# A planner that counts TensorE's instructions as ready some time behind their operands, in a hybrid attention and gated-MLP layer

## The chip, the cores and the metric

One core of one Trainium2 chip runs the whole layer as one program. The metric is the device time in microseconds (us), from the first to the last instruction with what lies around it. The engines are named as the profile names them: PE is TensorE (PEld its weight loads), DVE is VectorE, ACT is ScalarE, POOL is GpSimd, and SP issues the transfers. Each engine runs its own list of instructions strictly in order and waits for the others by semaphores.

## What is computed

The reference is one decoder layer over 2048 positions of 1024 numbers, in float32:

```
h = rmsnorm(x); qkv = h @ w_qkv
group A (4 heads): softmax(q1 k1) - lam * softmax(q2 k2), times v, per-head norm
group B (8 heads of 64): z = q k / 8;  beta = sigmoid(z);  1 - beta = sigmoid(-z)
     weight of key j = beta_j * product over later keys of (1 - beta);  out = weights @ v
x = x + rmsnorm(concat(A, B) @ w_o)
u = causal_conv3(rmsnorm(x) @ w_up);  x = x + rmsnorm((gelu(gate) * val) @ w_down)
```

The kernel keeps float32 accuracy on PE by splitting each operand into a rounded part (hi) and its rest (lo), and by three matmuls for hi*hi, hi*lo and lo*hi; in the heads two matmuls do where the hi and lo of one operand lie side by side.

## The kernel before

**The order of the work is made by a planner.** The program first records every piece of work as an `Op`, with its engine, an estimated duration, the operations it depends on and the buffers it takes. `Plan.run` (line 180 on) then plays this list through: at each moment it gives every idle engine the ready operation of the best priority whose buffers are free, and it writes out the instruction right there. So the planner's clock has no effect on the chip except one: it fixes the order in which the instructions of each engine stand. An operation counts as ready 200 ns (`LAT`) after the end of an operation of another engine that it needs, or 60 ns (`SAME`) after one of its own engine.

**The stages.** Up to about 750 us the program computes norms, the q/k/v projection (lines 603 and 606, tile `g`, weights `big`, activations `hT`) and the differential heads of group A. Each step of the projection is a row of six matmuls of 256 columns. Then come the stick-breaking heads of group B (`sb_stream`, line 929 on), in units of 512 queries by up to 512 keys, together with the rest of the projection as filler. The output projection (`wo_block`, line 1126 on, tiles `mt` and `g`, matmuls in line 1141) takes over as filler where the heads run out, and the MLP (`up` line 1266, `dn` line 1351) ends the program.

**One unit of group B** has four rows of 128 queries. For each row PE makes the scores `z` (line 959, with the mask of line 962 on the diagonal), ACT makes two sigmoids (lines 965 and 967), DVE a running product (the scan of line 973) and POOL the product of both (line 977). Then `tstep` transposes the four rows for one block of 128 keys on PE (line 989, four transposes into tile `t`), ACT or DVE rounds them (`thi`, lines 467 and 468), DVE takes the rest (`tlo`, line 996), and PE multiplies both by v into tile `o` (line 1012, first the `thi`, then the `tlo`). There are two buffers each for `t`, `thi` and `tlo`, so the transposes after next can be placed only behind the matmul that reads the present `tlo`.

Of the kernel before, what the change touches and what calls it, by code (L numbers as in the profile page):

```python
# [70 lines left out]


class Op:
    __slots__ = ("ways", "eng", "bufs", "prio", "left", "ready", "succ", "start", "end", "nbytes", "what")

    def alt(self, eng, dur, fn):

# [75 lines left out]
class Plan:  # L153
# [6 lines left out]
    QUEUE = 3000.0  # L160

    def __init__(self):
        self.ops, self.now = [], 0.0

    def op(self, eng, dur, fn, deps=(), bufs=(), lead=0.0, nbytes=0, what=None):
        o = Op()
        o.ways, o.eng, o.nbytes, o.what = {eng: (dur, fn)}, None, nbytes, what
        o.bufs = list(dict.fromkeys(bufs))
        for b in o.bufs:
            b.left += 1  # L170
            b.tag.ops.append(o)
        o.prio = (self.now - lead, len(self.ops))
        o.left, o.ready, o.succ, o.start, o.end = 0, 0.0, [], None, None
        for d in dict.fromkeys(deps):
            d.succ.append(o)
            o.left += 1
        self.ops.append(o)
        return o

    def run(self):  # L180
# [15 lines left out]
        while events:  # L196
# [9 lines left out]
            while again:  # L206
                again = False
                for e in engines:
# [6 lines left out]
                    for i, o in enumerate(ready[e]):  # L215
                        if any(b.held > t and b.by != e for b in o.bufs):
                            continue
                        new = [b for b in o.bufs if b.mem is None]
                        got = []
                        for b in new:  # L220
                            if not b.tag.fits(b):
                                break
                            b.tag.take(b)
                            got.append(b)
                        if len(got) < len(new):
                            for b in got:
                                b.tag.undo(b)
                            continue
                        for a in o.ways:
                            ready[a].remove(o)  # L230
                        dur, fn = o.ways[e]
                        o.eng = e
                        again = True
                        left -= 1
                        fn()
                        o.start = t
                        if e == "SP":
                            dma = max(dma, t + 1600) + o.nbytes / 250.0
                            o.end = dma + 1300
                            busy[e] = t + 475  # L240
                        else:
                            o.end = t + dur
                            busy[e] = o.end if e is not None else t
                        if busy[e] > t:
                            at(busy[e], "n", None)
                        for s in o.succ:
                            s.left -= 1
                            s.ready = max(s.ready, o.end + (self.SAME if list(s.ways) == [e] else self.LAT))
                            if s.left == 0:
                                at(s.ready, "r", s)  # L250
                        for b in o.bufs:
                            b.left -= 1
                            b.done = max(b.done, o.end)
                            if b.tag.bank and b.left:
                                b.held, b.by = o.end + self.BANK, e
                                at(b.held, "n", None)
                            if b.left == 0:
                                at(b.done + 100, "f", b)
                        break
# [7 lines left out]
def layer_kernel(  # L267
# [412 lines left out]
    def load_kv(g, c):  # L680
        cs = slice(c * 512, (c + 1) * 512)
        kt, v = buf("k"), buf("v")
        tiles = (2 * c, 2 * c + 1)
        assert all(kstore[g, i] and vstore[g // 2, i] for i in tiles)
        ok = load(lambda: f32(kt.t), kd[g][:, :, cs], 1 << 19, (kt,), [o for i in tiles for o in kstore[g, i]],
                  what="kload")
        ov = load(lambda: f32(v.t), vd[g // 2][g % 2, c], 1 << 19, (v,),
                  [o for i in tiles for o in vstore[g // 2, i]], what="vload")
        kv[g, c] = (kt, v, ok, (ov,))
# [728 lines left out]
    run(with_setup(qkv_steps(0, 2, 4)))  # L1418
    load_q(0, 0)
    load_kv(0, 0)  # L1420
    for mark, p, i0, i1 in (((0, 2), 0, 4, 6), ((0, 4), 0, 6, 8),
# [4 lines left out]
        run(merge(until(heads, *mark), qkv_steps(p, i0, i1)))  # L1426
    wo_weights()
    run(merge(until(heads), chain.from_iterable(wo_block(b) for b in range(8))))
    for b in range(8, NB):
        run(wo_block(b))  # L1430
    ffn_all()
    plan.run()

# [35 lines left out]
```

## Time and profile before

| | |
|---|---|
| median of 3 runs | 3116.48 us (3113.1 to 3118.24) |
| the profiled execution | 3117.43 us, its span 3115.6 us |
| PE busy | 2999.2 us, 96% |
| DVE busy | 2231.4 us, 72% |
| ACT, POOL busy | 1437.6 us (46%), 932.5 us (30%) |

The shares are means over stages that differ: DVE is idle much of the MLP and nearly full in group B. The profile also names, for each idle stretch of an engine, the instruction that ended it. A matmul's record can be longer than the time that it costs, because matmuls overlap.

### The profile page before, as it was taken

How to read it: one execution, taken by the hardware profiler on the slowest of the kernel's cores; microseconds unless marked ns; L12 is line 12 of the kernel's file. 1: busy time of each engine (PE TensorE's matmuls, PEld its weight loads, DVE VectorE, ACT ScalarE, POOL GpSimd, SP SyncE). 2: the span in 40 equal slices, each digit the busy share in tenths (PEclk: the TensorE clock that was granted, in tenths of full speed). 3: DMA queues.
4: the chain of work that ended last, by engine and by line, in shares of the span. 5: the costliest groups of instructions: out<-in, count | busy, mean ns of one | idle time of the engine just before them, and what ended most of it. 6: DMA issues, size and time to landing. Idle time of an engine off the chain costs nothing. (4 is left out here: it accounts for less than half of the span.)

```text
span 3115.6 us, 46750 instructions
## 1 busy us (share of the span) xinstructions
PE 2999.2 (96%) x16840; PEld 2586.1 (83%) x16840; DVE 2231.4 (72%) x4230; ACT 1437.6 (46%) x2873; POOL 932.5 (30%) x1008
## 2 busy tenths in 40 slices
PE   7999999999989998989999999999999999999998
PEld 7898999999878887867777888888888888888887
DVE  4658878897999898999755764377734776267742
ACT  4434545555676676766653433233422433233321
POOL 1011002002686675755422111033301332023310
PEclk9999999999999999999999999999999999999999
DMA  7775657655634355532263333343344333343332
GB/s 245 263 216 163 189 157 200 179 142 169 188 112 146 116 162 177 159 107 94 92 220 130 100 101 116 117 134 95 95 128 142 96 101 105 115 140 101 95 122 81
DMA packets 383965, 437.01 MB, mean 140 GB/s; under 512 B 20112, under 2 KB 311796, under 8 KB 373492
## 3 DMA queue, kind: packets, MB, share of 16 engines
q1 hardware_dynamic: 383732, 434.02, 46.1%
q8 instruction: 132, 2.16, 0.3%
q14 instruction: 101, 0.83, 0.1%
HBM read 333.27 MB, written 100.67 MB: 139 GB/s over the span
## 5 line engine op out<-in xcount | busy, mean ns | idle before, releaser
L1266 PE MATMUL pu<-fh,fhi 128*128 128x512 f32 x2816 | 868.2, 389 | 0.0
L1266 PEld LDWEIGHTS pu<-fh,fhi 128*128 128x128 f32 x2816 | 528.9, 188 | 110.4
L462 DVE TENSOR_TENSOR flo<-fraw,fhi 128x1024 fp32r<-128x1024 f32 x190 | 237.5, 1250 | 504.3 <-ACT fhi L459 504.0
L1266 PE MATMUL pu<-fh,flo 128*128 128x512 f32 x1408 | 548.2, 389 | 0.0
L977 POOL TENSOR_TENSOR ring_w<-ring_w,ring_a 128x512 f32<-128x512 f32 (+2 forms) x320 | 411.6, 1297 | 238.1 <-DVE ring_a L973 127.6
L459 ACT CAST fhi<-fraw 128x1024 fp32r<-128x1024 f32 x254 | 267.3, 1053 | 419.2 <-PE py L1351 248.0
L606 PE MATMUL g<-hT,big 128*128 128x256 f32 x3072 | 448.7, 288 | 8.1 <-DVE st L625 4.2
L1351 PE MATMUL py<-fhi,gt 128*128 128x512 f32 x1408 | 440.8, 393 | 0.0
L606 PEld LDWEIGHTS g<-hT,big 128*128 128x128 f32 x3072 | 412.2, 192 | 22.7 <-DVE st L625 5.6
L973 DVE TENSOR_TENSOR_SCAN ring_a<-ring_a 128x513 f32<-128x513 f32 (+2 forms) x320 | 408.0, 1295 | 7.4 <-ACT ring_a L965 6.6
L467 ACT CAST thi<-t 128x512 fp32r<-128x512 f32 (+3 forms) x422 | 215.5, 518 | 255.3 <-PE t L989 127.1
L1351 PEld LDWEIGHTS py<-fhi,gt 128*128 128x128 f32 x1408 | 264.3, 188 | 66.0
L1266 PEld LDWEIGHTS pu<-fh,flo 128*128 128x128 f32 x1408 | 264.4, 188 | 55.4
L460 POOL TENSOR_TENSOR flo<-fraw,fhi 128x1024 fp32r<-128x1024 f32 x74 | 186.0, 2514 | 356.8 <-ACT fhi L459 201.2
L1351 PE MATMUL py<-flo,gt 128*128 128x512 f32 x704 | 280.9, 399 | 0.0
L1290 POOL TENSOR_TENSOR gt<-fy,gt 128x512 fp32r<-128x512 f32 x88 | 117.3, 1334 | 515.7 <-ACT gt L1289 491.2
L1279 DVE SCALAR_TENSOR_TENSOR fy<-fu,cw,fy 128x512 f32<-128x512 f32 x176 | 241.2, 1371 | 6.2
L384 POOL TENSOR_TENSOR sm<-sm,neghalf 128x2 f32<-128x2 f32 (+1 forms) x72 | 79.2, 1099 | 535.7 <-DVE sm L382 503.4
L603 PE MATMUL g<-big,hT 128*128 128x256 f32 x1536 | 229.0, 289 | 3.3 <-POOL big L460 1.5
L603 PEld LDWEIGHTS g<-big,hT 128*128 128x128 f32 x1536 | 210.1, 195 | 11.1 <-POOL big L460 2.0
L996 DVE TENSOR_TENSOR tlo<-t,thi 128x512 fp32r<-128x512 f32 (+1 forms) x320 | 188.1, 593 | 31.0 <-ACT thi L467 30.5
L965 ACT ACTIVATE ring_a<-z 128x512 f32<-128x512 f32 (+2 forms) x320 | 178.0, 557 | 30.1 <-PE z L959 15.7
(166 smaller groups left out, 4984.3 us busy)
## 6 DMA issues: line engine op xcount, KB each, us to landing
fraw<-in_w_up_dram SPq DMA_DIRECT2D x176, 512.0 KB, 3.9
hT<-hd SPq DMA_DIRECT2D x64, 1024.0 KB, 6.5
fraw<-in_w_down_dram SPq DMA_DIRECT2D x88, 512.0 KB, 3.7
q<-qd SPq DMA_DIRECT2D x128, 256.0 KB, 4.3
hd<-hT SPq DMA_DIRECT2D x16, 1024.0 KB, 5.1
qd<-st SPq DMA_DIRECT2D x128, 128.0 KB, 3.2
kd<-st SPq DMA_DIRECT2D x128, 128.0 KB, 2.5
vd<-st SPq DMA_DIRECT2D x64, 256.0 KB, 3.6
```

What stands on the lines that cost most here:

```text
L459: "ACT", c_act(n) + 42, lambda: nc.scalar.copy(hi(), raw()))
L460: o2 = op("POOL", c_pool(n), lambda: nc.gpsimd.tensor_tensor(lo(), raw(), f32(hi()), ALU.subtract), (o1,), bufs, lead, what="split").alt(" ...
L462: "DVE", c_dvs(n), lambda: nc.vector.tensor_tensor(lo(), raw(), f32(hi()), ALU.subtract))
L467: return op("ACT", c_act(n), lambda: nc.scalar.copy(dst(), src()), deps, bufs, what=what).alt("DVE", c_dvp(n), lambda: nc.vector.tensor_co ...
L603: nc.tensor.matmul(ps.t[:, cs], hk[:, b, c * P:(c + 1) * P], wv[:, a, k, :], start=first, stop=last)
L606: nc.tensor.matmul(ps.t[:, cs], wv[:, a, k, c * P:(c + 1) * P], hk[:, b, :], start=first, stop=last)
L973: nc.vector.tensor_tensor_scan(gr, gr, gr, 1.0 if cb is None else cb[0].t[:, 0:1], ALU.mult, ALU.bypass)
L977: o = op("POOL", c_pool(w), lambda: nc.gpsimd.tensor_tensor(be.t[:, 0:w], be.t[:, 0:w], gm.t[:, 1:w + 1], ALU.mult), (o1, o2), (be, gm), w ...
L996: ol = op("DVE", c_dvp(n), lambda: nc.vector.tensor_tensor(lo.t[:, sl], ps.t[:, sl], f32(hi.t[:, sl]), ALU.subtract), (oh,), (ps, hi, lo), ...
L1266: nc.tensor.matmul(ps.t, w3(w)[:, k, :], h.t[:, a, k, :], start=(k == 0 and i == 0), stop=(k == KD - 1 and i == 2))
L1279: nc.vector.scalar_tensor_tensor(y.t, u.t[:, 1:TT + 1], cw[:, 1, f:f + 1], y.t, ALU.mult, ALU.add)
L1351: nc.tensor.matmul(ps.t, gt.t[:, a, j * P:(j + 1) * P], wt.t[:, ms], start=(m == 0 and i == 0), stop=(m == NFT - 1 and i == 2))
```

## The change

While the operations from the fifth block of the first projection pass to the end of the output projection are recorded, each operation of PE carries a slack of 1200 ns. In the planner's clock it counts as ready 1400 ns, not 200 ns, after the end of an operation of another engine, transfers included, that it needs. The engines and the planner's durations are as before, and so is all that is computed; the MLP's operations carry no slack.

```diff
@@ class Op
-    __slots__ = ("ways", "eng", "bufs", "prio", "left", "ready", "succ", "start", "end", "nbytes", "what")
+    __slots__ = ("ways", "eng", "bufs", "prio", "left", "ready", "succ", "start", "end", "nbytes", "what", "slack")
@@ class Plan
-        self.ops, self.now = [], 0.0
+        self.ops, self.now, self.slack = [], 0.0, 0.0
...
+        o.slack = self.slack if eng == "PE" else 0.0
...
-                            s.ready = max(s.ready, o.end + (self.SAME if list(s.ways) == [e] else self.LAT))
+                            s.ready = max(s.ready, o.end + (self.SAME if list(s.ways) == [e] else self.LAT + s.slack))
@@ layer_kernel
     load_q(0, 0)
     load_kv(0, 0)
+    plan.slack = 1200.0
...
     for b in range(8, NB):
         run(wo_block(b))
+    plan.slack = 0.0
     ffn_all()
```

Line numbers of the changed kernel are one higher from line 174 on. What follows is the order of the instructions in the two programs; it holds no times. The first place is in the first third of group B, on PE, behind the 328th transpose of line 989. Before:

```order
L989 MATMUL t_146<-ident,ring_w 128x128 x4
L1012 MATMUL o_218<-thi_185,v_178 128x128
L1012 MATMUL o_218<-tlo_187,v_178 128x128
L989 MATMUL t_145<-ident,ring_w 128x128 x4
L1012 MATMUL o_218<-thi_184,v_174 128x512
L1012 MATMUL o_218<-tlo_186,v_174 128x512
L1012 MATMUL o_218<-thi_185,v_174 128x512
L989 MATMUL t_146<-ident,ring_w 128x128 x4
L1012 MATMUL o_218<-tlo_187,v_174 128x512
L989 MATMUL t_145<-ident,ring_w 128x128 x4
```

The same place in the changed program:

```order
L990 MATMUL t_146<-ident,ring_w 128x128 x4
L1013 MATMUL o_218<-thi_185,v_178 128x128
L604 MATMUL g_148<-big_153,hT_159 128x256 x6
L607 MATMUL g_147<-hT_160,big_152 128x256 x6
L604 MATMUL g_148<-big_153,hT_159 128x256 x6
L1013 MATMUL o_218<-tlo_187,v_178 128x128
L607 MATMUL g_147<-hT_160,big_152 128x256 x6
L990 MATMUL t_145<-ident,ring_w 128x128 x4
L1013 MATMUL o_218<-thi_184,v_174 128x512
L607 MATMUL g_147<-hT_161,big_152 128x256 x6
L1013 MATMUL o_218<-tlo_186,v_174 128x512
L607 MATMUL g_147<-hT_161,big_152 128x256 x6
```

Rows of the projection now stand between the two products and ahead of the next transposes, where nothing stood before.

The second place is later in group B, on PE, behind the 688th transpose. Before, the filler of the projection still lasts there:

```order
L989 MATMUL t_146<-ident,ring_w 128x128 x4
L1012 MATMUL o_218<-thi_184,v_175 128x512
L959 MATMUL z_217<-k_170,q_179 128x512 x2
L606 MATMUL g_147<-hT_159,big_154 128x256 x6
L1012 MATMUL o_218<-tlo_186,v_175 128x512
L606 MATMUL g_147<-hT_159,big_154 128x256 x6
L989 MATMUL t_145<-ident,ring_w 128x128 x4
L1012 MATMUL o_218<-thi_185,v_175 128x512
L606 MATMUL g_147<-hT_158,big_154 128x256 x6
L1012 MATMUL o_218<-tlo_187,v_175 128x512
L606 MATMUL g_147<-hT_158,big_154 128x256 x6
```

In the changed program it is used up:

```order
L990 MATMUL t_146<-ident,ring_w 128x128 x4
L1013 MATMUL o_218<-thi_184,v_175 128x512
L1013 MATMUL o_218<-tlo_186,v_175 128x512
L990 MATMUL t_145<-ident,ring_w 128x128 x4
L1013 MATMUL o_218<-thi_185,v_175 128x512
L1013 MATMUL o_218<-tlo_187,v_175 128x512
L990 MATMUL t_146<-ident,ring_w 128x128 x4
L1013 MATMUL o_218<-thi_184,v_175 128x512
L960 MATMUL z_215<-k_170,q_179 128x512 x2
```

Transposes and products follow each other there without anything between. The third place is on DVE, near the first one, at the 101st `tlo` (a row named SCALAR_TENSOR_TENSOR on `ring_a` is the scan). Before:

```order
L996 TENSOR_TENSOR tlo_186<-t_146,thi_184 128x512
L973 SCALAR_TENSOR_TENSOR ring_a<-ring_a 128x257
L996 TENSOR_TENSOR tlo_187<-t_145,thi_185 128x512
L973 SCALAR_TENSOR_TENSOR ring_a<-ring_a 128x385
L996 TENSOR_TENSOR tlo_186<-t_146,thi_184 128x512
L625 TENSOR_TENSOR st_165<-g_148,st_165 128x4x64
L635 SCALAR_TENSOR_TENSOR st_164<-g_147,st_164 128x256
L996 TENSOR_TENSOR tlo_187<-t_145,thi_185 128x512
```

The same place in the changed program:

```order
L997 TENSOR_TENSOR tlo_186<-t_146,thi_184 128x512
L974 SCALAR_TENSOR_TENSOR ring_a<-ring_a 128x257
L974 SCALAR_TENSOR_TENSOR ring_a<-ring_a 128x385
L469 CAST st_164<-g_148 128x4x64
L626 TENSOR_TENSOR st_164<-g_148,st_164 128x4x64
L997 TENSOR_TENSOR tlo_187<-t_145,thi_185 128x512
L997 TENSOR_TENSOR tlo_186<-t_146,thi_184 128x512
L997 TENSOR_TENSOR tlo_187<-t_145,thi_185 128x512
```

The scans moved together ahead of three `tlo` that now follow each other with no scan between. Counted over the two whole orders, at the same points of group B (so many transposes of line 989 done), PE has done by then:

| transposes of 1088 | projection matmuls of 4608, before | after | output projection matmuls of 768, before | after |
|---|---|---|---|---|
| 128 | 3594 | 3648 | 0 | 0 |
| 544 | 4170 | 4566 | 0 | 0 |
| 872 | 4608 | 4608 | 0 | 36 |
| 1088 | 4608 | 4608 | 432 | 492 |

The scores `z` stand at 136, 428, 666 and 768 matmuls before, and at 142, 428, 668 and 768 after. Before the first of these points PE does nearly the same work in both, with single rows that change places. On DVE, between the 40th and the 160th `tlo`, there are 10 more roundings `thi` of 512 columns, 16 more rests `st` of the projection, 3 more `big` rests and 8 fewer scans; between the 160th and the 260th, 3 more `thi`, 18 fewer `st`, 6 fewer `big` rests and 3 more scans. Over the whole program 15 roundings `thi` of 512 columns move from ACT to DVE. In the MLP 17 of the weights' rests `flo` move from DVE to POOL.

## Rows read from the trace of the kernel before

**Rows 1.** Windows: busy time and instructions of each engine in seven stretches.

```profile
core 0: us, PE busy (x) PEld busy (x) DVE busy (x) ACT busy (x) POOL busy (x), PEclk, DMA share, GB/s
150.00:750.00 600.00, 592.88 (x4569) 568.15 (x4568) 491.70 (x1640) 300.63 (x660) 61.09 (x68) 1.00 0.62 179
750.00:868.00 118.00, 109.74 (x796) 101.80 (x795) 103.40 (x146) 74.62 (x175) 75.01 (x96) 0.99 0.59 175
868.00:1137.00 269.00, 244.98 (x1586) 213.10 (x1585) 252.24 (x326) 185.75 (x413) 190.35 (x268) 0.97 0.41 125
1137.00:1360.00 223.00, 197.29 (x1276) 169.73 (x1274) 210.36 (x284) 158.49 (x358) 146.86 (x204) 0.98 0.54 165
1360.00:1558.40 198.40, 184.81 (x959) 151.21 (x960) 164.43 (x232) 119.72 (x294) 99.14 (x135) 0.98 0.29 95
1558.40:1690.00 131.60, 125.17 (x561) 101.11 (x560) 70.33 (x117) 56.52 (x143) 33.62 (x36) 0.97 0.56 182
1690.00:3115.60 1425.60, 1416.76 (x6192) 1161.10 (x6190) 856.31 (x1239) 476.51 (x678) 309.14 (x177) 1.00 0.37 111
```

**Rows 2.** Windows of line 989's transposes alone (PE, PEld, clock, DMA).

```profile
868.00:1137.00 269.00, 68.87 (x419) 51.60 (x417) 0.97 0.41 125
1137.00:1360.00 223.00, 54.38 (x328) 39.25 (x327) 0.98 0.54 165
1360.00:1558.40 198.40, 33.83 (x217) 26.96 (x217) 0.98 0.29 95
```

**Rows 3.** Waits, 868 to 1137 us: total us, times, longest.

```profile
PE o L1012 <- DVE tlo L996: 13.8, 21, 2.1
DVE tlo L996 <- ACT thi L467: 12.6, 13, 1.7
```

**Rows 4.** Waits, 1137 to 1360 us.

```profile
PE o L1012 <- DVE tlo L996: 13.7, 14, 2.9
DVE tlo L996 <- ACT thi L467: 9.9, 11, 1.9
```

**Rows 5.** Timeline, 1206 to 1215 us: start, us, what [idle before it <-releaser].

```profile
1208.43 0.76 PE L1049 MATMUL t<-ident,mix 128*128 128x128 f32 x4 [1.78 <-DVE tlo L996]
...
1211.12 1.39 PE L606 MATMUL g<-hT,big 128*128 128x256 f32 x6
1211.56 0.69 DVE L996 TENSOR_TENSOR tlo<-t,thi 128x512 fp32r<-128x512 f32 x1 [1.59 <-ACT thi L467]
```

**Rows 6.** Chain that ended last, from 1690 us on: start, us, what.

```profile
1695.75 198.60 PE pu L1266 x876
```

**Rows 7.** DVE's groups by shape, 868 to 1360 us: busy, mean ns | idle before.

```profile
L973 DVE TENSOR_TENSOR_SCAN ring_a<-ring_a 128x513 f32<-128x513 f32 x155 | 226.9, 1477 | 2.0 <-ACT ring_a L965 1.5 <-POOL ring_w L977 0.2
...
L625 DVE TENSOR_TENSOR st<-g,st 128x256 fp32r<-128x256 f32 x16 | 6.5, 408 | 0.0
...
L462 DVE TENSOR_TENSOR big<-raw,big 128x512 fp32r<-128x512 f32 x6 | 5.5, 935 | 0.0
L468 DVE CAST thi<-t 128x512 fp32r<-128x512 f32 x8 | 5.4, 682 | 2.0 <-PE t L989 2.0
```

**Rows 8.** Windows of 10 us in group B, columns as in Rows 1.

```profile
940.00:950.00 10.00, 10.00 (x72) 9.23 (x71) 9.40 (x13) 7.27 (x17) 7.68 (x12) 1.00 0.72 226
...
1310.00:1320.00 10.00, 8.80 (x48) 6.32 (x45) 10.00 (x13) 9.62 (x22) 9.94 (x11) 1.00 0.74 170
1320.00:1330.00 10.00, 8.31 (x40) 6.70 (x39) 9.97 (x14) 7.23 (x17) 10.00 (x15) 0.83 0.24 68
1330.00:1340.00 10.00, 7.70 (x46) 5.85 (x47) 10.00 (x16) 7.28 (x21) 5.54 (x8) 1.00 0.28 79
```

**Rows 9.** Waits of PE, 150 to 750 us.

```profile
PE g L606 <- DVE st L625: 3.3, 3, 1.9
...
PE o L886 <- DVE tlo L735: 1.3, 2, 0.9
```

**Rows 10.** Source line 1266: duration min/median/max, first and last start us.

```profile
L1266 PE MATMUL pu<-fh,fhi x2816: 387/389/628, 1608.4 to 2982.9; 128*128 128x512 f32 x188
```

## The prediction

> **What bounds the kernel now.** I read the windows by stage first [rows 1]. Three regimes stand there. From 150 to 750 us PE is busy 592.9 of 600 us, and from 1690 us on 1416.8 of 1425.6: both stages are bound by PE, and the chain of waits confirms it for the MLP, where PE's own matmuls follow each other for 198.6 us without a wait [rows 6]. Between them, in group B, PE has gaps: 24.0 us of the 269 from 868 to 1137 us, 25.7 of the 223 up to 1360, 13.6 of the 198.4 up to 1558.4. But DVE is the fuller engine there: 252.2 of 269 and 210.4 of 223, that is 94% in both. So PE's gaps are mostly not the loss; the loss is what DVE stands idle, 16.8 and 12.6 us.
>
> Next I looked at who waits for whom. PE's largest wait in both stretches is that of the second product on `tlo`, 13.8 and 13.7 us, and DVE's is that of `tlo` on the rounding `thi`, 12.6 and 9.9 us [rows 3, 4]. They are two ends of one loop, and one place shows how it closes: PE stands 1.78 us behind a `tlo`, does its transposes late, and at 1211.56 us DVE has stood 1.59 us for the `thi` of these transposes [rows 5]. But in between, at 1211.12, PE is not waiting, it works on filler. So DVE can starve for two reasons: PE stood still before the transposes, or PE was busy with filler.
>
> The transposes of line 989 give a common measure for the two orders: 416, 328 and 216 of them make the three stretches, and the trace counts 419, 328 and 217 there (the edges fall inside a group) [rows 2]. So the table of counts in the section on the change can be laid on these stretches.
>
> **The change part by part.** It adds and removes no instruction of PE. It moves filler forward in group B, since a transpose or product that counts as ready 1.2 us later lets the planner put a row of the projection ahead of it; the two places on PE in the change show this, and the counts say how much. The price of a matmul is 198.60 us over 876, or 0.2267 us for 512 columns [rows 6]; a projection matmul of 256 columns is half, 0.1134 us.
>
> *150 to 750 us: 0.* PE has nothing to gain: 7 us idle, and of its waits only 1.3 us is on a rest `tlo`, the kind that the slack reaches [rows 1, 9]. Bounds -2 and +2.
>
> *750 to 868 us: +2.* By the 128th transpose PE has done 54 more projection matmuls (6.1 us) and three more pairs of scores (at most 1.4 us). That makes 109.7 + 7.5 = 117.2 us in a stretch of 118. DVE has 8 more scans there, about 10 us (five of 1.477 and three narrower), and some 2 us less of roundings: 103.4 + 8 = 111. Both just fit. Bounds 0 and +7.5 (nothing fits); near the lower one, since both sums are still below 118.
>
> *868 to 1137 us: +13, the term that decides.* Of projection matmuls the old order has 4170 - 3594 = 576 here, the new one 4566 - 3648 = 918: 342 more, 38.8 us, less 1.4 for the scores done before. DVE gets 10 roundings (6.8 us), 16 rests `st` (6.5), 3 `big` rests (2.8) and 8 scans fewer (-10): +6, to 258 us [rows 7]. So DVE still fits into 269, and PE does not: 245.0 + 37.4 = 282.4. Lower bound 0: PE's busy time counts stretched records, and at the densest place, 72 matmuls in 10 us [rows 8], the 1586 + 336 matmuls would take 267 us. Upper bound +37: all 24 us of idle stay on top of 282.4. I take 282, +13, PE's busy time with no idle left: in that densest place PE shows none, and DVE drops to 9.40 of 10 us [rows 8], which is how a stretch bound by PE looks. The third place in the change fits it: three `tlo` stand there without a scan between, so DVE waits for the filler on PE and not the other way round.
>
> *1137 to 1360 us: -16.* Now the projection is used up: 42 of its matmuls are left in place of 438 (-44.9 us), 36 of the output projection come forward (+8.2). PE goes from 197.3 to 160.6 us and can't bind. DVE loses 18 `st` (-7.3) and 6 `big` rests (-5.6), and gets 3 roundings (+2.0) and 3 scans (+4.4), with smaller ones about -8: 202 us. Bounds: 202 (-21) if DVE is never idle, 214.6 (-8) if its 12.6 idle us stay. The old program shows what DVE does without filler of the projection: from 1310 to 1340 us it is busy 29.97 of 30 us [rows 8]. I still leave 5 us of idle time, since the wait of the second product on `tlo` stays in this order with nothing between: 207.
>
> *1360 to 1558 us: +2.* Here stand 456 matmuls of the output projection in place of 432, +5.4 us on PE's 184.8, with 13.6 idle. Bounds 0 and +6.
>
> *1558 to 1690 us: -11.* At the last transpose 60 more matmuls of the output projection are done, 13.6 us, with eight more transposes behind them, about 1 us. PE is busy 125.2 of 131.6 us, so what is done already is nearly all saved. Bounds -14.5, and 0 if the MLP's first matmuls wait for their transfers anyway. The cover for these is what is left of the output projection, 276 matmuls or 62.6 us, more than the 50 us that the old program takes from 1558.4 to its first `up` at 1608.4 [rows 10]; so I take three quarters.
>
> *The MLP: 0.* POOL gets 17 rests `flo` more, and is busy 309 of 1425.6 us; PE covers them.
>
> Sum: 0 + 2 + 13 - 16 + 2 - 11 + 0 = -10. The profiled execution took 3117.4 us, 0.9 above the median of its runs; so I expect **3107 us**, 9 us under the median. A difference of 0.2%, about 6 us, is what a measurement of this kernel can tell.
>
> **A rule that speaks against it.** In the slices with little filler at 1310 to 1340 us PE is busy 7.7 to 8.8 of 10 us; the granted clock is 1.00 in two of them and 0.83 in one [rows 8], so the engine spent some of that one at 1.2 GHz and the rest at 2.4. The Trainium skill (TensorE: Matmul & The Clock Gate, Part 1: The HAM clock gate) says that the half clock is the engine's default and that only sustained work lifts it. By that rule PE, with 160.6 us of work in 207, could fall back; the trace agrees in the one slice and not in its neighbours. What it would take is a rival below.
>
> **The rivals.** *DVE keeps the pace everywhere.* If PE's busy time before is mostly stretched records, 868 to 1137 us grows by DVE's 6 us alone; if DVE's idle time in the next stretch stays, that one shrinks by only 8; with +2, +2 and half of the last term (-5) the sum is -3: 3114 us, no change. For it speaks that DVE is at 94% in both stretches; against it the 38.8 us of added matmuls on an engine with 24 idle.
>
> *PE binds early and nothing is given back (the other side).* Filler between transposes makes `tlo` wait, as at 1211.56 us [rows 5]. If half of PE's idle time stays, 868 to 1137 becomes 294.4 (+25), 750 to 868 becomes 123 (+5), the next stretch gives only its lower bound of 8, 1360 to 1558 takes +4, and the end gives 7, since the transfers of the MLP set its start: +19, 3136 us. It decides from the point where the first two terms together pass 25, which is what the others give in my sum (16 + 11 - 2). Against it: where filler is dense now, PE has no idle time.
>
> *The clock falls where the filler is gone.* PE's 160.6 us fill the 207 when 46 us of them, 29%, run at half speed. If half does, the stretch takes 241 us, +18 in place of -16: 3117 + 24 = 3141 us with my other terms. One slice in three at 0.83 is far from it.
>
> That the change does nothing is excluded: the two orders differ in thousands of rows.
>
> **How the numbers follow.** My forecast has 0.49, and its own range is 3094 to 3118; DVE's pace 0.23, from 3108 to 3123; the slow case 0.25, from 3122 to 3145; the clock 0.03. The lower end takes +7 for +13, -21 for -16 and -14.5 for -11, which is 3092; the upper end takes in the lower half of the slow case: 3092 to 3131. Faster by over 0.2% (below 3110): 0.35 of the forecast and 0.06 of DVE's case, 0.41. Within 0.2%: 0.14 and 0.16, 0.30. Slower: 0.01 of DVE's case, the slow case and the clock, 0.29.
>
> **What would show it.** Marked by the same counts of transposes, the trace after should show 416 transposes from the 129th to the 544th in about 282 us with PE over 97% busy and DVE near 91%; the next 328 in about 207 us, with DVE over 96%, PE near 78% and a granted clock not much under 0.97; the first `up` some 50 us behind the last transpose, and fewer output projection matmuls beside it. PE's wait on `tlo` should go from the first of these stretches and remain or grow in the second. Wrong would be: PE's share below 93% in the first with a longer stretch (the loop closed in another way), the second stretch at 215 us or more, or the end not shorter by 8 us.

## The result and the profile after

The changed kernel takes 3167.9 us in the median of 4 runs (3165.0 to 3170.9), the kernel before 3116.7 beside it: a ratio of 1.0166, with a 95% interval of 1.0148 to 1.0184. It is 51 us slower, 61 us above the forecast and outside its range of 3092 to 3131 us.

The counts of transposes of line 989 (now 990) mark the same work in both traces. Times between the marks, in us, worked out from the starts of these transposes, of the first `up` matmul and the end:

| from, to | before | after | difference | forecast |
|---|---|---|---|---|
| start to 1st transpose | 757.5 | 750.9 | -6.6 | 0 |
| 1st to 128th | 110.5 | 118.3 | +7.8 | +2 |
| 128th to 544th | 268.7 | 317.8 | **+49.1** | +13 |
| 544th to 872nd | 223.3 | 242.3 | **+19.0** | -16 |
| 872nd to 1088th | 198.4 | 199.6 | +1.2 | +2 |
| 1088th to first `up` | 50.0 | 48.6 | -1.4 | -11, with the next |
| first `up` to end | 1507.3 | 1491.2 | -16.0 | |

The first two rows belong together: the forecast cut at 750 us, the table at the first transpose, which comes 6.6 us earlier. Up to the 128th transpose the change is 1.2 us longer. Each time here is from one profiled run, and some us of scatter lie in it: e7 below, which has the changed kernel's order as far as the 544th transpose, comes to its first transpose at 754.6 us.

The windows of the changed kernel by these marks answer to [rows 1]; the columns are those of that group, and the last line runs from the first `up` on:

```profile
150.00:750.00 600.00, 596.39 (x4599) 570.09 (x4598) 492.85 (x1637) 305.18 (x665) 67.43 (x71) 1.00 0.62 179
750.00:869.00 119.00, 110.10 (x795) 102.09 (x795) 110.18 (x149) 76.45 (x177) 84.97 (x104) 0.99 0.57 169
869.00:1187.00 318.00, 286.67 (x1923) 257.75 (x1921) 265.15 (x348) 185.25 (x415) 173.89 (x266) 0.95 0.57 176
1187.00:1429.00 242.00, 183.27 (x919) 144.55 (x917) 209.72 (x263) 151.54 (x335) 151.33 (x207) 0.87 0.21 58
1429.00:1629.00 200.00, 190.35 (x991) 156.98 (x990) 166.21 (x238) 124.29 (x311) 99.61 (x134) 0.98 0.33 108
1677.50:3168.70 1491.20, 1482.35 (x6489) 1214.87 (x6487) 922.58 (x1284) 504.53 (x740) 370.64 (x205) 1.00 0.37 113
```

The kernel before has, from its first `up` on:

```profile
1608.40:3115.60 1507.20, 1496.28 (x6545) 1225.68 (x6543) 898.53 (x1308) 511.10 (x759) 327.80 (x195) 1.00 0.37 113
```

In the third line PE is busy 286.7 us and DVE 265.2; the forecast had 282 and 258. In the fourth DVE has 209.7, forecast 202 to 207. So the work was sized about right there (DVE 7 us short in the first), and what came on top is idle time, and it lies on *both* engines in the same stretches: 318 - 286.7 = 31 us of PE and 53 us of DVE in one, 59 and 32 us in the next. Neither engine is full. On DVE the account closes: of the 49 us, 13 are more work and 36 more idle time; of the 19, all is idle time.

The windows of the transposes alone, as [rows 2], show that the stretches hold the same transposes:

```profile
869.00:1187.00 318.00, 67.31 (x420) 50.25 (x418) 0.95 0.57 176
1187.00:1429.00 242.00, 61.01 (x329) 44.90 (x327) 0.87 0.21 58
```

The waits of the changed kernel from 869 to 1187 us, as [rows 3]:

```profile
DVE tlo L997 <- ACT thi L468: 38.7, 24, 6.2
...
PE g L607 <- DVE st L640: 9.0, 4, 3.1
PE o L1013 <- DVE tlo L997: 8.2, 10, 2.8
```

and from 1187 to 1429 us, as [rows 4]:

```profile
DVE tlo L997 <- ACT thi L468: 24.1, 17, 3.2
PE o L1013 <- DVE tlo L997: 22.5, 21, 3.2
...
PE t L1050 <- DVE tlo L997: 12.5, 6, 3.2
```

DVE's wait of `tlo` for `thi` went from 12.6 and 9.9 us to 38.7 and 24.1. PE's wait for `tlo` fell in the first stretch (13.8 to 8.2), since filler now lies in it, and rose in the second (13.7 to 22.5). PE's largest wait in the first stretch is a new one, 9.0 us of rows of filler that wait for DVE to read an earlier row out of its `g` buffer (`st`). A row that waits at the head of PE's list also holds up the transposes behind it. The timeline of the changed kernel at one of the longest waits (start, us, what, idle before and its releaser):

```profile
908.39 1.27 DVE L997 TENSOR_TENSOR tlo<-t,thi 128x512 fp32r<-128x512 f32 x2
...
908.52 0.98 PE L607 MATMUL g<-hT,big 128*128 128x256 f32 x6 [2.69 <-DVE st L640]
...
910.06 1.48 PE L607 MATMUL g<-hT,big 128*128 128x256 f32 x6
...
911.34 0.63 PE L1013 MATMUL o<-tlo,v 128*128 128x512 f32 x1
...
911.77 1.48 PE L607 MATMUL g<-hT,big 128*128 128x256 f32 x6
...
913.05 0.74 PE L990 MATMUL t<-ident,ring_w 128*128 128x128 f32 x4
...
913.83 0.59 ACT L468 CAST thi<-t 128x512 fp32r<-128x512 f32 x1 [3.17 <-PE t L990]
...
914.45 0.69 DVE L997 TENSOR_TENSOR tlo<-t,thi 128x512 fp32r<-128x512 f32 x1 [4.79 <-ACT thi L468]
...
914.58 0.39 PE L1013 MATMUL o<-tlo,v 128*128 128x512 f32 x1
...
914.81 0.87 PE L607 MATMUL g<-hT,big 128*128 128x256 f32 x6
...
915.53 0.60 PE L990 MATMUL t<-ident,ring_w 128*128 128x128 f32 x4
...
916.84 0.69 DVE L997 TENSOR_TENSOR tlo<-t,thi 128x512 fp32r<-128x512 f32 x1 [1.70 <-ACT thi L468]
```

And in windows, with the columns of [rows 1]:

```profile
905.00:908.50 3.50, 0.82 (x6) 0.55 (x5) 3.18 (x5) 1.17 (x2) 1.92 (x5) 1.00 0.96 300
908.50:910.00 1.50, 1.48 (x11) 1.45 (x12) 1.16 (x2) 0.03 (x1) 0.92 (x1) 0.98 0.92 377
910.00:913.50 3.50, 3.50 (x17) 3.34 (x16) 0.00 (x0) 0.66 (x1) 0.00 (x0) 0.52 0.56 177
```

The reader is to follow one round. PE stands 2.69 us for DVE's `st`, and starts at 908.52. DVE ends two `tlo` at 909.7 us; its next entry is a third `tlo`, with no scan in between. For that one PE must transpose again, and in the order written out these transposes stand behind the product that reads an earlier `tlo` and behind rows of filler. They come at 913.05, the rounding follows, and DVE starts at 914.45 after 4.79 idle us. The next round repeats it with 1.70. First PE stands while DVE works, then DVE stands while PE works without a gap. From 910 to 913.5 us PE's granted clock is 0.52, so nearly all of that is at 1.2 GHz, behind its idle time: the rows of six take 1.48 us in place of 0.88. At this place filler and the low clock both lengthen DVE's wait; the runs below tell how much of the whole loss is theirs.

### The profile page after: what moved, and what is told of

Its sections match the earlier page's. It is cut to its first block, busy times and chain, and to the rows that moved or that the text cites. A ratio compares the mean times of both kernels' runs of the same rounds, so it can differ in the third digit from the quotient of the medians.

```text
span 3168.7 us, 46884 instructions
## 1 busy us (share of the span) xinstructions
PE 3018.0 (95%) x16840; PEld 2599.0 (82%) x16840; DVE 2277.6 (72%) x4223; ACT 1440.0 (45%) x2864; POOL 975.9 (31%) x1024
## 4 chain that ended last, share of the span: by engine, by line
PE 81%; DVE 10%; issue 3%; ACT 2%; POOL 1%; DMA 1%; SPq 0%; POOLq 0%; DVEq 0%; ACTq 0%
PE pu L1267 30%; PE py L1352 16%; PE g L607 10%; PE g L604 5%; PE g L1142 5%; DVE ring_a L974 5%; PE z L704 4%; PE o L1013 2%; PE t L990 2%; PE t L722 2%; DVE tlo L997 2%; PE z L960 2%; PE o L882 1%; PE o L887 1%; PE o L881 1%
## 5 line engine op out<-in xcount | busy, mean ns | idle before, releaser
L463 DVE TENSOR_TENSOR flo<-fraw,fhi 128x1024 fp32r<-128x1024 f32 x173 | 215.8, 1248 | 481.3 <-ACT fhi L460 480.7
L978 POOL TENSOR_TENSOR ring_w<-ring_w,ring_a 128x512 f32<-128x512 f32 (+2 forms) x320 | 393.8, 1242 | 289.0 <-DVE ring_a L974 156.2
L607 PE MATMUL g<-hT,big 128*128 128x256 f32 x3072 | 450.5, 289 | 14.8 <-DVE st L640 13.4
L974 DVE TENSOR_TENSOR_SCAN ring_a<-ring_a 128x513 f32<-128x513 f32 (+2 forms) x320 | 423.7, 1344 | 10.7 <-ACT ring_a L966 9.2
L461 POOL TENSOR_TENSOR flo<-fraw,fhi 128x1024 fp32r<-128x1024 f32 x91 | 228.1, 2506 | 410.2 <-ACT fhi L460 265.6
L468 ACT CAST thi<-t 128x512 fp32r<-128x512 f32 (+3 forms) x408 | 207.5, 516 | 305.3 <-PE t L990 172.9
L1280 DVE SCALAR_TENSOR_TENSOR fy<-fu,cw,fy 128x512 f32<-128x512 f32 x176 | 275.5, 1565 | 6.2
L385 POOL TENSOR_TENSOR sm<-sm,neghalf 128x2 f32<-128x2 f32 (+1 forms) x72 | 87.2, 1211 | 548.8 <-DVE sm L383 514.5
L1291 POOL TENSOR_TENSOR gt<-fy,gt 128x512 fp32r<-128x512 f32 x88 | 125.6, 1428 | 406.7 <-ACT gt L1290 390.3
L990 PE MATMUL t<-ident,ring_w 128*128 128x128 f32 x1088 | 183.4, 286 | 18.2 <-DVE os L1035 9.5
```

The source lines that it names most:

```text
L461: o2 = op("POOL", c_pool(n), lambda: nc.gpsimd.tensor_tensor(lo(), raw(), f32(hi()), ALU.subtract), (o1,), bufs, lead, what="split").alt(" ...
L463: "DVE", c_dvs(n), lambda: nc.vector.tensor_tensor(lo(), raw(), f32(hi()), ALU.subtract))
L607: nc.tensor.matmul(ps.t[:, cs], wv[:, a, k, c * P:(c + 1) * P], hk[:, b, :], start=first, stop=last)
L974: nc.vector.tensor_tensor_scan(gr, gr, gr, 1.0 if cb is None else cb[0].t[:, 0:1], ALU.mult, ALU.bypass)
L978: o = op("POOL", c_pool(w), lambda: nc.gpsimd.tensor_tensor(be.t[:, 0:w], be.t[:, 0:w], gm.t[:, 1:w + 1], ALU.mult), (o1, o2), (be, gm), w ...
L990: nc.tensor.transpose(ps.t[:, jj * P:(jj + 1) * P], rows[jj][0].t[:, kb * P:(kb + 1) * P], ident)
```

## The theories

- **A, the filler.** Drawn forward, it makes PE too full in the first stretch and leaves it too empty in the second. This is the prediction's own picture with larger numbers.
- **B, the later place.** Transposes and products that stand later on PE cost by themselves; **D** in later runs is B for the products alone.
- **C, the round of two buffers.** In the plan a group (transposes, `thi`, `tlo`, two products) holds one of two pairs of `thi` and `tlo` until its second product is done. The slack makes that hold longer in the plan's clock, the plan's round of two groups gets too long for the pace, and the order that it writes out has scans in bunches on DVE, then `tlo` in bunches, each waiting for the round. Counted over the orders, 56 `tlo` stand in runs of three or more without a scan before, and 80 after (in the two traces, up to the last scan, 51 and 77).
- **The clock.** The granted clock is 0.87 in the second stretch, a mean of parts at 1.2 GHz and parts at 2.4, and was 0.98 before. It can be the cause of the long stretch or a result of PE's idle time.

The comparison kernels ran on the same chip as their runs of the kernel before (medians 3116.0 to 3116.8). "Heads" in the table is the time from the 128th to the 872nd transpose in the profiled run, against 492.0 before; "end" that from the first `up`, against 1507.3. The planner's name `av` covers the products of group A too, so in e1 and e9 these carry the slack as well; "heads" begins behind them.

| run | us, median | ratio, 95% interval | heads | end |
|---|---|---|---|---|
| the change | 3167.9 | 1.0166 [1.0148, 1.0184] | +68.2 | -16.0 |
| e1 products only | 3154.2 | 1.0123 [1.0108, 1.0138] | +59.7 | -15.3 |
| e2 transposes only | 3107.8 | 0.9972 [0.9962, 0.9981] | +3.0 | 0.0 |
| e3 slack, filler tied | 3159.4 | 1.0139 [1.0122, 1.0156] | +38.1 | -15.5 |
| e4 filler tied, no slack | 3112.8 | 0.9992 [0.9982, 1.0001] | -8.8 | 0.0 |
| e5 filler early, no slack | 3109.6 | 0.9982 [0.9972, 0.9991] | +6.5 | 0.0 |
| e6 half filler | 3156.2 | 1.0129 [1.0113, 1.0146] | +50.5 | -16.1 |
| e7 busy products | 3171.0 | 1.0175 [1.0158, 1.0192] | +68.5 | -16.0 |
| e8 slack from output projection | 3106.8 | 0.9970 [0.9960, 0.9979] | +0.8 | -16.0 |
| e9 first product only | 3119.5 | 1.0011 [1.0002, 1.0020] | +28.6 | -15.3 |
| e10 second product only | 3166.4 | 1.0161 [1.0146, 1.0177] | +73.7 | -21.3 |
| e11 three pairs | 3089.8 | 0.9916 [0.9901, 0.9931] | -23.3 | +9.0 |
| e12 three pairs, no slack | 3090.1 | 0.9919 [0.9902, 0.9935] | -30.8 | +13.5 |
| e13 two pairs, smaller ring | 3148.9 | 1.0107 [1.0091, 1.0122] | +55.1 | -16.1 |
| e14 third pair unknown to the plan | 3153.9 | 1.0118 [1.0103, 1.0133] | +55.0 | -16.0 |
| e15 slack 600 | 3132.8 | 1.0050 [1.0034, 1.0067] | +27.6 | +0.1 |
| e16 transposes, then output projection | 3097.1 | 0.9936 [0.9921, 0.9951] | +0.4 | -16.0 |

## Which part of the slack: e1 to e4

All diffs are against the changed kernel. e1 and e2 give the slack to one kind of operation:

```diff
-        o.slack = self.slack if eng == "PE" else 0.0
+        o.slack = self.slack if eng == "PE" and what == "av" else 0.0   (e1)
+        o.slack = self.slack if eng == "PE" and what == "T" else 0.0    (e2)
```

> Slack of 1200 ns on the products with v alone. By the order, the projection is then used up as early as in the full change: 4566 of its matmuls by the 544th transpose (before 4170, full change 4566). Theory A, filler drawn forward makes TensorE too full first and too empty later: 3155 to 3175 us. Theory B, it is the later place of transposes and finishing steps themselves that costs: at most half of the 51 us, 3117 to 3143 us.

> Slack of 1200 ns on the transposes of lines 721 and 989 alone. The filler stands as before: 4170 projection matmuls by the 544th transpose. Theory A: no change, 3111 to 3123 us. Theory B: a good part of the loss stays, 3135 us or more.

The products carry the loss: with the slack on them alone 59.7 of the 68.2 us in the heads are there, with it on the transposes alone 3.0, and e2 is 0.3% faster than the kernel before, its profile gaining 10.9 us ahead of the 128th transpose. By the totals e1 (3154.2) is 1 us under the range of A and far above that of B, and e2 (3107.8) is under both. e1 also draws the filler forward as far as the change does (4566 matmuls by the 544th transpose), so it does not yet tell A from the rest. e3 keeps the slack and ties each filler row, in the plan, to the newest transposes; e4 has the tie without slack.

```diff
+            if "lastT" in mem:
+                deps.append(mem["lastT"])
             st["last"] = op("PE", 6 * c_mm(256), go
...
-            chain_["t"] = o
+            chain_["t"] = mem["lastT"] = o
...
-    plan.slack = 1200.0
+    plan.slack = 0.0   (e4 only)
```

> Full slack, but each row of the projection must in the plan follow the newest transposes recorded ahead of it (both on TensorE, so nothing waits on the chip that did not). Filler can't be drawn forward: 4062 projection matmuls by the 544th transpose, fewer than before. Theory A: the loss is gone, 3100 to 3125 us. Theory B: the loss stays, 3150 us or more.

> The same tie as in the gated run, with no slack: 4062 projection matmuls by the 544th transpose. Theory A: near the kernel before, 3105 to 3125 us, and the gated run with slack within 10 us of it. Theory B: this one near 3117 and the gated run with slack some 40 us above it.

In both, only 4062 filler matmuls stand ahead of the 544th transpose (4170 before). With the slack the kernel still takes 3159.4 us, without it 3112.8. So with the filler tied the slack still costs 46.6 us in all and 46.9 in the heads (+38.1 against -8.8), and with the filler free 68.2 in the heads: the loss does not need filler drawn forward, which adds some 20 us. What e3 loses besides, 13.4 us from the 872nd to the 1088th transpose, is the tie's, for e4 loses 14.5 there.

## Filler, capacity, clock: e5 to e8

e5 draws the filler forward without any slack (4500 matmuls by the 544th transpose):

```diff
-    plan.slack = 1200.0
...
-                            ((5, 2), 3, 0, 3), ((6, 0), 3, 3, 6), ((6, 2), 3, 6, 8),
-                            ((6, 3), 4, 0, 2), ((7, 0), 4, 2, 4), ((7, 1), 4, 4, 6), ((7, 2), 4, 6, 8)):
+                            ((5, 0), 3, 0, 4), ((5, 2), 3, 4, 6), ((5, 3), 3, 6, 8),
+                            ((6, 0), 4, 0, 5), ((6, 2), 4, 5, 8)):
...
+    run(until(heads, 7, 2))
     wo_weights()
```

> No slack at all; instead the rows of projection passes 3 and 4 are recorded earlier among the heads, so that 4500 of the 4608 filler products stand ahead of the 544th transpose (before 4170, after 4566), while only 36 of the tlo subtractions stand in runs of three or more with no scan between (before 56, after 80). Theory A (the filler that is drawn forward costs the time): 3145 to 3160 us, with 128 to 544 at least 25 us longer. Theory C (the bunched list on VectorE costs it): 3112 to 3130, with 128 to 544 at most 12 us longer and most of that returned behind it.

It came out at 3109.6, below both ranges: A falls as a cause by itself. From the 128th to the 544th transpose it takes 275.3 us, 6.5 more than before, with PE busy 264.9 of 275 us. Its waits there:

```profile
DVE tlo L997 <- ACT thi L468: 9.7, 15, 1.6
...
PE o L1013 <- DVE tlo L997: 6.0, 11, 1.1
```

That is the full PE that the prediction had in mind, and it exists where the slack is absent. e6 takes the capacity side from the other end:

```diff
                     for n, (a, b) in enumerate(((0, 0), (1, 0), (0, 1)) if is_v else ((0, 0), (0, 1), (1, 0))):
+                        if p >= 3 and n == 2 and k % 2 == 0 or p >= 3 and n == 1:
+                            continue
```

> The changed kernel's order unmoved; in projection passes 3 and 4 half of the six matmuls of each row are left out (parts of the low-order products, so those heads' values come out coarser), which takes some 65 us of TensorE's busy time out, most of it from the stretch between transposes 128 and 544. If TensorE's capacity there is the limit (theory A, and the prediction's own +13): 3100 to 3115, the stretch back to at most 275 us. Theory C (both engines stand in turns because of the order on VectorE): 3135 to 3155, the stretch still at least 290 us.

The window of e6 from the 128th to the 544th transpose:

```profile
872.00:1172.00 300.00, 242.66 (x1459) 206.43 (x1458) 265.73 (x350) 183.74 (x415) 175.31 (x266) 0.94 0.60 185
```

3156.2 us, just over C's range, and the stretch still takes 300.5 us though PE is busy only 242.7 of 300 there. Half of the filler was worth 17 us of the 49 in that stretch: PE's work is a part of the loss there and not the bulk. e7 adds work to PE in the second stretch:

```diff
-            o = op("PE", c_mm(n), lambda: go(hi, False), ...
+            def go_hi():
+                go(hi, False)
+                if 41 <= u < 65:
+                    for _ in range(3):
+                        nc.tensor.matmul(po.t[:, sl], v.t[:, kb, m * P:(m + 1) * P], hi.t[:, sl], start=False, stop=False)
+            o = op("PE", c_mm(n), go_hi, ...
```

> The changed kernel's order unmoved; in the last third of the wide heads each first product is issued four times instead of once (the results of those heads are wrong by that factor), which puts some 50 us of extra work on TensorE between transposes 544 and 872, where its granted clock was 0.87 on average. If the low clock alone makes that stretch long: the clock comes back to 0.97 or more there and the stretch falls from 242 to 225 to 235 us, in all 3150 to 3162. If the turns between the engines make it long (theory C): the clock comes back and the stretch stays within 5 us of 242 or grows by up to 15, in all 3163 to 3185.

The window of e7 from the 544th to the 872nd transpose:

```profile
1190.00:1434.00 244.00, 214.84 (x1203) 176.12 (x1203) 210.42 (x264) 152.40 (x339) 150.89 (x209) 0.98 0.20 57
```

PE's granted clock is 0.98 in place of 0.87, with 284 matmuls more, and the stretch takes 244.2 us in place of 242.3: the clock came back and the time didn't. The Trainium skill (TensorE: Matmul & The Clock Gate, Part 1: The HAM clock gate) has the half clock as the default that activity lifts; the trace agrees, 0.87 as the change left it and 0.98 with the added matmuls. But the added matmuls also stand in the rounds and lengthen them, so e7 alone could hide a gain by the clock. Three runs settle it without added work, between the 544th and the 872nd transpose, e3, e4 and e5:

```profile
1156.80:1397.80 241.00, 205.18 (x1379) 179.66 (x1378) 209.06 (x282) 151.31 (x343) 133.08 (x201) 0.98 0.51 152
1119.30:1342.50 223.20, 202.95 (x1376) 177.00 (x1375) 208.56 (x289) 152.90 (x339) 126.01 (x201) 0.99 0.52 164
1141.60:1364.80 223.20, 184.74 (x1004) 148.50 (x1002) 218.23 (x282) 159.49 (x353) 150.89 (x219) 0.91 0.30 88
```

With the slack the stretch is 241.0 us at a clock of 0.98 (e3), without it 223.2 at 0.99 (e4) and 223.2 at 0.91 (e5). The loss is there at the full clock and absent at a lower one, so the clock is not what sets this stretch. e8 starts the slack where the output projection is recorded:

```diff
-    plan.slack = 1200.0
...
+    plan.slack = 1200.0
     wo_weights()
```

> The slack begins only when the output projection is recorded, so that all of the wide heads' order stays that of the kernel before. Expected by the stage table of the earlier runs, where every version with slack on the last part ran 15 to 16 us shorter between the first up product and the end: 3098 to 3104. If that gain was only the order of the heads spilling over: 3114 to 3118.

3106.8 us (3099.8 to 3110.2), a little above the range; the 16.0 us at the end are there in full, with the heads as before. They are in part work that was moved: from the 872nd to the 1088th transpose e8 takes 7.2 us more than the kernel before.

## The round of two buffers: e9 to e16

e9 and e10 give the slack to the first or to the second of the two products of a group, whose operations get names of their own (`av`, `av2`):

```diff
-            chain_["av"] = op("PE", c_mm(n), lambda: go(lo, True), [ol, o], (po, lo, v), what="av")
+            chain_["av"] = op("PE", c_mm(n), lambda: go(lo, True), [ol, o], (po, lo, v), what="av2")
...
+        o.slack = self.slack if eng == "PE" and what == "av" else 0.0    (e9)
+        o.slack = self.slack if eng == "PE" and what == "av2" else 0.0   (e10)
```

> Slack on the first (thi) product of each group alone. In the plan its 1400 ns run beside the tlo subtraction (about 0.66 us) and the 200 ns behind it, so a group holds its thi and tlo buffers only some 0.5 us longer; 60 tlo subtractions stand in runs of three or more without a scan (before 56, after 80). Theory C (the plan's round of two buffers becomes too long, and VectorE's list comes in bunches): 3105 to 3125 us. Rival D (any later place of the products on TensorE costs): as with slack on both products, 3145 to 3160.

> Slack on the second (tlo) product of each group alone: a group holds its buffers the whole 1200 ns longer in the plan; 79 tlo subtractions stand in runs of three or more. Theory C: 3140 to 3160 us, with the waits of tlo for thi at least twice those of before between transposes 128 and 872. Rival D: about the same as with slack on the first product alone, within 10 us.

3119.5 and 3166.4 us, 47 apart: D falls. e9 lies in C's range, e10 6 us above it. The same 1200 ns cost 28.6 us in the heads on the first product, whose wait runs beside `tlo` in the plan, and 73.7 on the second, where they lengthen the hold of the pair in full. DVE's wait from the 128th to the 872nd transpose, of e9 and then of e10 (before 22.5 us):

```profile
DVE tlo L997 <- ACT thi L468: 31.4, 24, 2.9
```

```profile
DVE tlo L997 <- ACT thi L468: 73.5, 41, 4.6
```

e11 is the change whole with a third pair, e12 the same without slack:

```diff
-                    ("thi", 2), ("tlo", 2), ("mo", 1), ("ot", 1), ("os", 1), ("mix", 1),
+                    ("thi", 3), ("tlo", 3), ("mo", 1), ("ot", 1), ("os", 1), ("mix", 1),
...
-    T["w"] = Ring(8 * 1024)
+    T["w"] = Ring(7 * 1024 + 128)
...
-    plan.slack = 1200.0
+    plan.slack = 0.0   (e12 only)
```

> The change whole, with three thi and three tlo buffers in place of two (the ring of wide tiles gives up 3.5 KB a partition for them), so a third group may be under way while two wait out the slack; 56 tlo subtractions stand in runs of three or more, as before the change. Theory C: 3095 to 3125 us, most of the 50 us back. Rival D (later products cost by themselves): 3145 to 3165.

> Three thi and three tlo buffers as in the run beside it, and no slack anywhere. What three buffers are worth alone: if the round of two buffers also limits the kernel before, 3090 to 3110 us; if not, 3110 to 3125. Its list on VectorE is bunched as after (77 tlo subtractions in runs of three or more, 116 scans in runs): if such a list costs by itself, whatever the buffers, 3135 to 3155.

3089.8 and 3090.1 us, e11 5 us below C's range: with three pairs the slack costs nothing in all (7.5 us more in the heads, returned elsewhere), and both kernels are 26 us faster than the kernel before. The two windows of e11 between the 128th, 544th and 872nd transpose, and its waits in the first:

```profile
859.00:1112.00 253.00, 228.47 (x1525) 197.87 (x1524) 250.96 (x326) 180.88 (x404) 164.31 (x260) 0.99 0.39 121
1112.00:1327.00 215.00, 196.18 (x1342) 171.51 (x1341) 208.80 (x288) 157.00 (x352) 147.08 (x209) 1.00 0.57 174
```

```profile
PE t L990 <- DVE tlo L997: 16.6, 21, 2.5
...
DVE tlo L997 <- ACT thi L468: 1.4, 2, 1.2
```

DVE is busy 251.0 of 253 us: it fills the stretch now, and its wait for `thi` is nearly gone, also against the kernel before (12.6). One part of C falls with e12: its list on DVE is bunched like that of the change (77 `tlo` in runs of three or more), and it is fast. Whether the bunches cost anything beside a round of two pairs no run separates: where the round is long, in the change and in e10, the list is bunched too.

e13 is the change with the smaller ring and two pairs; e14 has its order row for row, while the chip's tiles rotate over three pairs:

```diff
+class Rot(Tag):
+    def take(self, b):
+        self.free.popleft()
+        b.mem = self.turn % 3
+        self.turn += 1
...
+    T["thi"], T["tlo"] = Rot(2), Rot(2)
```

> The change whole with the smaller ring that the third pair of buffers needed, but with two pairs: what the smaller ring alone does. If the third pair brought the time back: 3150 to 3185 us. If the smaller ring did it: 3085 to 3100.

> Every engine's order is that of the run beside it (two pairs, smaller ring), row for row; only the chip's tiles rotate over three pairs, of which the plan knows nothing. If the order that the plan wrote out is the cause (in it TensorE's transposes after next stand behind the second product, which waits for tlo, so that a free buffer is of no use): within 10 us of the run beside it. If the chip's two buffers are the limit: at least 30 us less.

3148.9 (1 us under the range) and 3153.9 us, and the same marks within 0.5 us in the profiles. A third pair that the plan does not know of is of no use: PE's next transposes still stand behind the product that waits for `tlo`. DVE's wait in e14 from the 128th to the 544th transpose (27.9 in e13):

```profile
DVE tlo L1010 <- ACT thi L481: 28.1, 19, 4.2
```

The window of e14 there:

```profile
872.00:1173.00 301.00, 273.08 (x1871) 244.89 (x1870) 265.72 (x346) 183.02 (x412) 162.93 (x256) 0.98 0.57 181
```

301 us at a granted clock of 0.98, against 269 at 0.97 before: in the first stretch too the loss does not need a low clock. So it is the written order, made under two pairs and a lengthened hold, that costs. Two things go with it. The smaller ring alone is worth 19 us under the slack (3167.9 to 3148.9), and why stays open. And the third pair also lets the planner leave filler back, 4110 projection matmuls by the 544th transpose in e11 against 4512 in e13, so some of their 59 us can be the filler's; by e3 and e4 its share in the heads was some 20 of 68 us. e15 and e16 ask how the loss grows, and what adds up:

```diff
-    plan.slack = 1200.0
+    plan.slack = 600.0   (e15)
```

> The change with a slack of 600 ns in place of 1200. In the plan a round of two groups is then some 0.6 us longer, not 1.2 or more; 66 tlo subtractions stand in runs of three or more (before 56, after 80). Theory C, a loss that grows once the round is longer than the pace of the scans allows: 3118 to 3145 us. If the loss went by the place of the products alone, in proportion to the slack: 3138 to 3148, half of the loss and half of the gain at the end.

3132.8 us: 27.6 of the 68.2 us in the heads at half the slack. That is inside C's range, but 40% at one half is too near to proportion to tell a threshold. By the estimates in the expectations the plan's hold grows by some 0.5 us in e9 and 1.2 in e10, and its round by 0.6 in e15; the heads lose 28.6, 73.7 and 27.6 us, so the loss goes roughly with the hold.

```diff
-        o.slack = self.slack if eng == "PE" else 0.0
+        o.slack = self.slack if eng == "PE" and (self.late or what == "T") else 0.0   (e16)
...
+    plan.late = True
     wo_weights()
```

> Slack on the transposes alone as far as the heads are recorded ahead of the output projection, on all of TensorE's operations from there to its end: the two parts that ran shorter. If they add up: 8 us and 10 to 16 us, 3092 to 3099. If both are the same gain: 3104 to 3109.

3097.1 us: the gains add up (8.6 in e2, 9.4 in e8), 19.7 us under the kernel before with the same two pairs.

## Why the prediction was wrong

- **150 to 750 us, 0, and 750 to 868 us, +2:** -6.6 and +7.8, together +1.2 up to the 128th transpose, as forecast. The split is only that of the first transpose; e8, without slack there, comes to it 4.5 us earlier too.
- **868 to 1137 us, +13, the step that failed first.** I took "PE's busy time with no idle left". The busy time was right (286.7 against 282), the "no idle left" wrong: 31 us of idle time stand on PE (24 before) and 53 on DVE (16.8 before), and the +49.1 lies above my upper bound of +37, for which all the old idle time stayed. I judged by the dense slices of the trace before [rows 8], in which products stood right behind their `tlo`. The change moves these products, and with them the transposes after next, which the plan can place only behind them. The section on the kernel said so, and I did not price it. e5 has filler nearly as dense without the moved products, and there the stretch grew by 6.5. My reading of [rows 5] hid it: the transposes at 1208.43 us are those of `mix`. Those that the `tlo` at 1211.56 needed are in the line below, ahead of the filler at 1211.12, so this wait is no case of PE busy with filler.
- **1137 to 1360 us, -16, the second:** +19.0. The work was again about as forecast on DVE (209.7), and on PE 23 us above (183.3 against 160.6; its records are longer at the low clock). I let 5 idle us stay on DVE; 32 did, 24.1 of them in waits of `tlo` for `thi`. I had named the waiting second product and taken it for small because it was 13.7 us before [rows 4].
- **1360 to 1558 us, +2:** +1.2, right.
- **The end, -11:** -1.4 - 16.0 = -17.4. The mechanism was right, 492 in place of 432 output projection matmuls done at the last transpose, and the size was too small. Most of what was saved appears behind the first `up`: 120 output projection matmuls are left there in place of 168, PE is busy 13.9 us less, and 2.1 us of its idle time go too. The other runs roughly follow the same count: 120 in e8 and e16 with -16.0, 168 in e2, e4 and e5 with 0, 96 in e10 with -21.3, and 216 in e11 and e12 with +9.0 and +13.5 (e3 fits least, 102 with -15.5).
- **The rivals:** "PE binds early and nothing is given back" had the sign, and its picture, half of PE's idle time staying, was nearest, but it priced 868 to 1137 us at +25 in place of +49 and let the next stretch gain 8. The clock did fall, to 0.87, and e3, e5 and e7 show that this is not what cost the time in that stretch.
- **The tests named ahead of the result** pointed at it: PE's share in the first stretch is 90% (286.7 of 318), below 93%, in a longer stretch, "the loop closed in another way"; and the second stretch passed 215 us. The third sign of being wrong, an end not shorter by 8 us, did not come.

The line of the kernel before that belongs to [rows 5]:

```profile
1209.85 1.05 PE L989 MATMUL t<-ident,ring_w 128*128 128x128 f32 x4
```

What should have decided stood in the diff: the planner's readiness also sets how long a pair is held. 1200 ns more on a hold of two pairs is overlap that the plan gives up, and more work for PE in between does not give DVE its next `tlo` sooner.

## What to carry to other kernels

A delay in a planner's clock changes more than the place of the delayed instruction: it lengthens the hold of every buffer that instruction frees, so ask for each delayed operation what it frees, how many of it there are, and which engine needs the next one. When two engines pass work back and forth through two buffers, price the round (here transposes, rounding, rest, product) and not the busy time of the fuller engine: in the first stretch the work was within 3% of the forecast, and the time 13% above it. And give a buffer to the planner, not only to the chip: the order made for a third pair was worth 59 us (e11 against e13), and a third pair that the plan did not know of nothing (e14).

## What the runs showed that was not expected

- A granted clock below full did not set the time of the second stretch: 241.0 us at 0.98 with the slack (e3), 223.2 at 0.91 without (e5). Single rows do get longer, 1.48 us for a row of six against 0.88 in the timeline above, and there DVE waited for them; over the stretch the round decided.
- The kernel before seems to have the same loss in small: with three pairs DVE's wait for `thi` over the heads falls from 22.5 us to 2.6 (e11) and 1.8 (e12), and the heads from 492.0 us to 468.7 and 461.2, with a granted clock of 1.00 (0.97 before). But e11 and e12 also have the smaller ring, and no run has it with two pairs and no slack; the gain of 26 us is not shown to be the third pair's alone.
